# A hybrid decoder step on one Trainium2 core: the list scheduler of layer B makes several passes

## The chip, the cores and the metric

The kernel runs on one core of a Trainium2 chip. The metric is the device time in microseconds of one execution, as the median of several runs. A profile of one further execution shows what each engine did: PE is TensorE, DVE is VectorE, ACT is ScalarE, POOL is GpSimd, and SP is SyncE, whose queue issues all the transfers of this kernel.

## What is computed

One inference step of two layers, for a prompt of 1024 tokens and 64 sample tokens (8 sequences of 8) beside it, with D = 1024. Layer A is a gated short convolution. Layer B is a gated DeltaNet with 8 heads of 128 x 128 state, scanned in chunks:

```
def gdn_mixer(u, conv_buf, s0, w_in, w_conv, a_log, dt_bias, norm_w, w_out):
    p = u @ w_in
    qkv, new_buf = causal_dwconv(p[..., :GDN_CONV_CH], conv_buf, w_conv)
    qkv = jax.nn.silu(qkv).astype(f32)
    ...
    q = l2norm(...); k = l2norm(...); v = ...
    beta = jax.nn.sigmoid(b)
    g = -jnp.exp(a_log) * jax.nn.softplus(a + dt_bias)
    o, S = gated_delta_rule(q, k, v, g, beta, s0)
    o = o * lax.rsqrt(jnp.mean(o * o, axis=-1, keepdims=True) + NORM_EPS) * norm_w
    return (o.reshape(...) * jax.nn.silu(z)) @ w_out, new_buf, S

def gated_delta_rule(q, k, v, g, beta, s0):      # per head and chunk
    L = where(causal, exp(G_i - G_j), 0);  A = where(strict, (k beta) k^T * L, 0)
    u, w = solve(I + A, [v beta, k beta exp(G)]);  attn = (q k^T) * L
    # scan over the chunks
    v_new = u - w @ S;  o = (q exp(G)) @ S + attn @ v_new
    S = S * exp(G_last) + kt^T @ v_new
```

After each layer stands x = layer_norm(ALPHA * x + gate * out).

## The kernel before

Wide products are made from three float32r matmuls: each operand is split into a high and a low part (`uh`, `ul` for the activations in three groups of 384, 384 and 320 columns; `wh`, `wl` for the weights), and hi*hi, lo*hi and hi*lo go into one PSUM bank. A unit of layer B is 24 such matmuls into a bank `g`. The weights of a unit come in halves through one raw buffer `wr`: a load, then two splits on ACT (`wh`) and on DVE (`wl`), then the next load.

Each head has two halves of 512 tokens, and each half is a chain (`prep`): transposes of k (`kq`), the sum of squares on ACT, a power on POOL and three small DVE steps for 1/norm, the normalised keys `kn`, their transpose `KN`, the products KN*KN and KN*kq, from which DVE makes `AT` and `att` with the decay matrix `Lt`. Then the triangular inverse is built in six levels of small matmuls in fp16: 12 products of `DH` and `AH`, 8 products with a unit matrix `id16` that turn a block (`flip`), 12 products of `YH` and `EH`, with DVE and ACT between them. The even and odd half use the banks `t0` and `t1`; their buffers are named with 0 and 1, and with 2 for the samples. A `scan` follows: for each of four chunks the products S*KN, R*E and vn*kt in bank `s`, each ended by one DVE step, and the two products of the output in bank `o`. `norm_out` sums squares, makes f = 1/norm in the same way (ACT, POOL, DVE), and PE transposes the scaled output (`s<-cons,qg`). The samples of a pair of heads go through `sample`: 32 small products of the stored state `S0` with the sample keys `vx`, in two rounds, each round after two loads `S<-in_s_dram`.

The decay matrices are made at the start of layer B (`gates`): `Gc` is transposed on PE, stored to `d_rows`, loaded back as broadcast rows into `rb` and `E`, put through Exp on ACT, stored to `d_L`, and loaded as `Lt`. Exp and Silu need different tables on ACT.

The output projection of layer B (`out_proj`) follows; its first products are put among the last scans.

What sets the order: the kernel's code calls each operation once, and `Plan.add` records it with its price (`Plan.price`: time on the engine, and time until others see the result), what it needs (`deps`) and what it must only follow (`behind`). PE instructions of one output go together as a unit. `Plan.arrange` then schedules the recorded middle of layer B: it gives each unit the length of the longest way to the end, steps through time, gives each of five queues (T = PE, V, A, G, D = SP) the ready unit with the longest way, and ties the queue's instructions in that order. `Plan.on` is set from `gates` to the end of the last head; layer A and the output projections are not recorded. The steps of the change are in `Plan.price`, `Plan.add` and `Plan.arrange`, and in a new `Plan.order`.

## Time and profile before

| | |
|---|---|
| median of 3 runs | 1360.61 us (1359.68 to 1361.13) |
| profiled execution, time | 1356.89 us |
| profiled execution, span | 1355.1 us |
| busy: PE / PEld / DVE / ACT / POOL | 97% / 88% / 61% / 48% / 15% |
| granted clock of PE, mean | 0.994 |

PE is busy nearly all the time. Matmuls are pipelined and their recorded ends overlap, so for PE the distance from one start to the next is read, and what it waits for before an instruction. The recorded middle of layer B lies between about 560 us and 1251 us of the span; layer A is ahead of it, the rest of the output projection behind it.

### The profile page before, as it was taken

The numbers are of one execution on the slowest core, as the hardware profiler recorded it, in microseconds if no ns is written. First come the engines' busy times: TensorE is split into PE (matmuls) and PEld (weight loads), VectorE is DVE, ScalarE is ACT, GpSimd is POOL, SyncE is SP. The second block draws the span as 40 slices with busy tenths as digits, with TensorE's granted clock in tenths as the row PEclk, the third lists the DMA queues.
The fourth block names the chain that finished last, engine by engine and source line by source line (L and its number), as shares of the span: only waits on it lengthen the run. The fifth ranks groups of instructions, "written<-read, shape, count | busy, mean of one in ns | idle before, by whom it ended". The sixth has DMA issues, their size and how long they took to land.

```text
span 1355.1 us, 27508 instructions
## 1 busy us (share of the span) xinstructions
PE 1309.0 (97%) x10631; PEld 1197.4 (88%) x10631; DVE 831.9 (61%) x2010; ACT 652.9 (48%) x1878; POOL 209.4 (15%) x326
## 2 busy tenths in 40 slices
PE   7999999999999999898999999999999999998997
PEld 5898889999999777798999899999999899996775
DVE  3444143244233688667866877787787667557687
ACT  3411212222221355478965768676776567445321
POOL 0011000000000144211121212130303102001041
PEclk9999999999999999999999999999999999999999
DMA  8735542221212332246331232222222224336852
GB/s 310 265 126 190 223 135 77 87 83 68 86 65 68 123 125 88 73 130 187 118 101 50 67 111 80 67 74 88 67 84 83 89 71 129 113 130 202 252 177 68
DMA packets 119023, 160.22 MB, mean 118 GB/s; under 512 B 21220, under 2 KB 74220, under 8 KB 116844
## 3 DMA queue, kind: packets, MB, share of 16 engines
q1 hardware_dynamic: 118892, 158.46, 36.3%
q8 instruction: 83, 1.36, 0.4%
q14 instruction: 48, 0.39, 0.1%
HBM read 123.61 MB, written 34.82 MB: 117 GB/s over the span
## 4 chain that ended last, share of the span: by engine, by line
PE 44%; DVE 7%; DMA 4%; ACT 2%; issue 1%; POOL 1%; SPq 0%; POOLq 0%; ACTq 0%; DVEq 0%
PE g L106 24%; PE t L106 13%; PE s L106 5%; PE o L106 3%; DVE acc L106 1%; DMA S<-in_s_dram 1%; DVE xt L106 1%; DVE wl L106 1%; DMA E<-d_rows 1%; DMA rb<-d_rows 1%; DMA wr<-in_wb_dram 0%; DMA wr<-d_y 0%; DVE Y L106 0%; POOL f1y L106 0%; DVE st L106 0%
## 5 line engine op out<-in xcount | busy, mean ns | idle before, releaser
L106 PE MATMUL g<-uh,wh 128*128 128x384 f32 (+3 forms) x1080 | 376.2, 352 | 1.1 <-DVE wh L106 0.8
L106 PE MATMUL g<-ul,wh 128*128 128x384 f32 (+3 forms) x1080 | 355.1, 332 | 0.0
L106 PE MATMUL g<-uh,wl 128*128 128x384 f32 (+2 forms) x1064 | 350.6, 333 | 0.2 <-DVE wl L106 0.2
L106 DVE TENSOR_TENSOR wl<-wr,wh 128x256 fp32r<-128x256 f32 (+1 forms) x225 | 133.6, 610 | 178.1 <-ACT wh L106 177.9
L106 ACT ACTIVATE wh<-wr 128x256 fp32r<-128x256 f32 (+2 forms) x227 | 109.3, 501 | 213.6 <-PE t L106 118.1
L106 PEld LDWEIGHTS g<-uh,wh 128*128 128x128 f32 (+1 forms) x1080 | 202.2, 187 | 6.1 <-issue 1.2
L106 PEld LDWEIGHTS g<-ul,wh 128*128 128x128 f32 (+1 forms) x1080 | 202.1, 187 | 2.8
L106 PEld LDWEIGHTS g<-uh,wl 128*128 128x128 f32 x1064 | 199.4, 188 | 2.7 <-DVE wl L106 0.5
L106 PE MATMUL t<-uh,wh 128*128 128x384 f32 (+3 forms) x540 | 177.7, 336 | 4.1 <-ACT uh L106 2.9
L106 PE MATMUL t<-ul,wh 128*128 128x384 f32 (+3 forms) x540 | 177.1, 335 | 0.1
L106 PE MATMUL t<-uh,wl 128*128 128x384 f32 (+2 forms) x532 | 173.7, 333 | 0.3 <-DVE wl L106 0.3
L106 DVE SCALAR_TENSOR_TENSOR acc<-xb,wbc,acc 128x512 f32<-128x512 f32 (+1 forms) x144 | 113.8, 792 | 19.1 <-ACT acc L106 18.5
L106 PEld LDWEIGHTS t<-uh,wh 128*128 128x128 f32 (+1 forms) x540 | 101.4, 188 | 16.0 <-issue 6.3
L106 PEld LDWEIGHTS t<-ul,wh 128*128 128x128 f32 (+1 forms) x540 | 101.8, 188 | 5.1 <-issue 2.1
L106 PEld LDWEIGHTS t<-uh,wl 128*128 128x128 f32 x532 | 100.3, 189 | 3.6 <-issue 0.8
L106 ACT ACTIVATE xb<-g 128x384 f32<-128x384 f32 (+4 forms) x122 | 49.7, 413 | 78.8 <-PE g L106 77.7
L106 ACT ACTIVATE EH<-t 128x256 f16<-128x256 f32 (+1 forms) x176 | 57.0, 365 | 5.4 <-PE t L106 4.7
L106 ACT ACTIVATE DH<-t 128x256 f16<-128x256 f32 (+1 forms) x128 | 46.6, 384 | 23.3 <-PE t L106 22.3
L106 PE MATMUL t<-DH,AH 128*128 128x64 f16 x1176 | 52.3, 193 | 1.5 <-DVE DH L106 0.9
L106 PEld LDWEIGHTS <-AH 128*128 128x128 f16 x1176 | 43.4, 98 | 9.9 <-issue 7.2
L106 PEld LDWEIGHTS <-EH 128*128 128x128 f16 x1120 | 41.9, 98 | 9.6 <-issue 4.3
L106 ACT ACTIVATE YH<-Y 128x256 f16<-128x256 f32 (+1 forms) x104 | 41.7, 402 | 17.1 <-DVE Y L106 15.2
(361 smaller groups left out, 2377.7 us busy)
## 6 DMA issues: line engine op xcount, KB each, us to landing
wm<-in_wm_dram SPq DMA_DIRECT2D x16, 1024.0 KB
wr<-in_wb_dram SPq DMA_DIRECT2D x64, 256.0 KB
wr<-in_wa_dram SPq DMA_DIRECT2D x62, 256.0 KB
wm<-in_wm_dram SPq DMA_DIRECT2D x16, 512.0 KB
wr<-d_y SPq DMA_DIRECT2D x32, 256.0 KB
S<-in_s_dram SPq DMA_DIRECT2D x32, 256.0 KB
d_y<-cs SPq DMA_DIRECT2D x8, 544.0 KB
wr<-in_wo_dram SPq DMA_DIRECT2D x16, 256.0 KB
```

The source lines that it names most:

```text
L106: r = call(*args, **kw)
```

## The change

Four things change, all in the planner; the set of operations that the kernel issues stays the same, apart from the table loads of ACT that the order asks for.

1. `arrange` no longer makes one pass. It ranks the units by the longest way, schedules (`order`), schedules the reversed graph from the end with the start times of that pass as ranks, takes the starts of the reversed pass as the next ranks, and so on, six times; the forward pass with the smallest planned end is used.
2. On T, `order` keeps to the class of the last unit (fp16, or anything else) while a ready unit of that class has a rank at most `STAY` = 4.0 below the best one. A change from fp16 to another class is priced at 0.08 (before: 0.078 for a change from any other class to float32r).
3. A transfer is priced at size / rate on its queue, with the rate by the length of contiguous runs, and 2.0 until it is seen (before: 0.06 on the queue, 2.0 + size / 300e3 until seen).
4. Small operations on V and G are priced a little higher; a scale operand on A a little lower; `bn_stats` gets a price of its own, though no recorded part uses it.

```
+    STAY = 4.0
+    PASSES = 6
...
-    V = ((1, 0.155), (128, 0.345), (256, 0.41), (512, 0.69), (1112, 1.34))
-    G = ((1, 0.25), (128, 0.4), (512, 1.3), (1112, 2.65))
+    V = ((1, 0.18), (128, 0.345), (256, 0.41), (512, 0.69), (1112, 1.34))
+    G = ((1, 0.3), (128, 0.4), (512, 1.3), (1112, 2.65))
...
         if kind == "D":
-            return 0.06, 2.0 + min(x.free_size() for x in outs + ins) * P * 4 / 3e5
+            size = min(x.shape[0] * x.free_size() for x in outs + ins) * 4
+            run = min((x.ap[-1][1] if x.ap[-1][0] == 1 else 1) for x in outs + ins) * 4
+            rate = 340e3 if run >= 2048 else 300e3 if run >= 1024 else 200e3 if run >= 512 else max(8e3, run * 300.0)
+            return max(0.06, size / rate), 2.0
+        if kind == "V" and name == "bn_stats":
+            return 0.05 + 0.00106 * ins[0].free_size(), 0.115
...
+            wide = 2 if x.dtype == F32R else x.dtype != F16
...
+    def order(cls, kinds, cost, edges, rank):
...
+            if k == "T":
+                if (kinds[top[1]][1] == 0) != (state[k] == 0):
+                    top = min((x for x in w if (kinds[x[1]][1] == 0) == (state[k] == 0) and x[0] <= top[0] + cls.STAY), default=top)
+                if kinds[top[1]][1] and not state[k]:
+                    t += 0.08
+                state[k] = kinds[top[1]][1]
...
+        best = None
+        for _ in range(cls.PASSES):
+            r = cls.order(kinds, cost, ahead, rank)
+            if best is None or r[0] < best[0]:
+                best = r
+            start = cls.order(kinds, cost, back, {u: t + cost[u][0] for u, t in r[1].items()})[1]
+            rank = {u: t + cost[u][0] for u, t in start.items()}
```

Three places of PE's order, all in the last head.

PE, the last fp16 products of the last sample inverse (bank `t0`, buffers with 2) among a scan step (`s`) and products of the output projection (`t1`), before:

```order
L106 LDWEIGHTS EH2_16393
L106 MATMUL t0_16514<-YH2_16489,EH2_16393 128x64
L106 MATMUL s_16563<-R_16542,E1_16335 128x128
L106 MATMUL t1_16879<-uh0_99,wh_16829 128x512
L106 LDWEIGHTS DH2_16392
L106 MATMUL t0_16554<-id16_76,DH2_16392 128x64
L106 MATMUL t1_16879<-ul0_102,wh_16829 128x512
L106 LDWEIGHTS DH2_16392
L106 MATMUL t0_16554<-id16_76,DH2_16392 128x64
L106 MATMUL t0_16618<-S0_16595,vx_16591 32x128
```

and the same two products `t0_16554` after:

```order
L106 MATMUL o_16286<-vn_16475,att0_15263 128x128
L106 MATMUL s_16498<-vn_16475,kt0_15150 128x128
L106 LDWEIGHTS DH2_16392
L106 MATMUL t0_16554<-id16_76,DH2_16392 128x64
L106 LDWEIGHTS DH2_16392
L106 MATMUL t0_16554<-id16_76,DH2_16392 128x64
L106 MATMUL t0_16618<-S0_16595,vx_16591 32x128
```

Three runs of fp16 products, each followed by another class, stand in the first piece; the second has one.

PE, what stands between the first and the second round of the last sample state products (`t0_16618`, `t0_16665`), before:

```order
L106 MATMUL t0_16618<-S0_16597,vx_16591 32x128
L106 MATMUL s_16577<-vn_16565,kt1_15302 128x128
L106 MATMUL g_16840<-uh0_99,wh_16823 128x512
L106 MATMUL g_16841<-uh0_99,wh_16823 128x512
L106 MATMUL g_16840<-ul0_102,wh_16823 128x512
L106 MATMUL g_16841<-ul0_102,wh_16823 128x512
L106 MATMUL g_16840<-uh0_99,wl_16824 128x512
L106 MATMUL o_16539<-S_16500,qg1_15233 128x128
L106 MATMUL o_16539<-vn_16565,att1_15391 128x128
L106 MATMUL s_16603<-cons_75,qg0_15108 128x128 x4
L106 MATMUL g_16841<-uh0_99,wl_16824 128x512
L106 MATMUL g_16840<-uh0_99,wh_16823 128x512
```

and after, the last eleven rows ahead of the second round:

```order
L106 MATMUL t1_16334<-EH1_15447,YH1_16259 64x64
L106 MATMUL g_16841<-uh0_99,wl_16824 128x512
L106 MATMUL g_16840<-uh1_100,wh_16823 128x512
L106 MATMUL g_16841<-uh1_100,wh_16823 128x512
L106 MATMUL s_16563<-R_16542,E1_16335 128x128
L106 MATMUL g_16840<-ul1_103,wh_16823 128x512
L106 MATMUL g_16840<-uh1_100,wl_16824 128x512
L106 MATMUL g_16841<-ul1_103,wh_16823 128x512
L106 MATMUL g_16841<-uh1_100,wl_16824 128x512
L106 MATMUL s_16577<-vn_16565,kt1_15302 128x128
L106 MATMUL t0_16665<-S0_16637,vx_16591 32x128
```

Ahead of these, behind the first round, the second order also has one scan product, the 12 products and 8 flips of a level of `t1`, five output products `g` and three more among the 12 small products of `t1_16334`.

PE, from the last output product of the last scan (`o`) to the transposes of the last norm (`s_16776`), before:

```order
L106 MATMUL o_16539<-vn_16702,att1_15391 128x128
L106 MATMUL s_16708<-vn_16702,kt1_15302 128x128
L106 MATMUL t1_16879<-ul0_102,wh_16829 128x512
L106 MATMUL t1_16878<-uh0_99,wl_16830 128x512
L106 MATMUL t1_16879<-uh0_99,wl_16830 128x512
L106 MATMUL t1_16878<-uh1_100,wh_16829 128x512
L106 MATMUL t1_16879<-uh1_100,wh_16829 128x512
L106 MATMUL t1_16878<-ul1_103,wh_16829 128x512
L106 MATMUL t1_16879<-ul1_103,wh_16829 128x512
L106 MATMUL t1_16878<-uh1_100,wl_16830 128x512
L106 MATMUL t1_16879<-uh1_100,wl_16830 128x512
L106 MATMUL s_16776<-cons_75,qg1_15233 128x128 x4
```

and after:

```order
L106 MATMUL o_16539<-vn_16702,att1_15391 128x128
L106 MATMUL s_16708<-vn_16702,kt1_15302 128x128
L106 MATMUL t1_16878<-uh1_100,wl_16830 128x512
L106 MATMUL t1_16879<-uh1_100,wl_16830 128x512
L106 MATMUL s_16776<-cons_75,qg1_15233 128x128 x4
```

Nine products of the output projection stand between the two before, and two after; the other seven now stand ahead of the scan's last steps.

## Rows read from the trace of the kernel before

**Rows 1.** Stages: length, busy us (count) of PE, PEld, DVE, ACT, POOL, then clock.

```profile
588.00:700.00 112.00, 107.02 (x1034) 101.01 (x1035) 86.11 (x227) 97.30 (x252) 19.65 (x37) 1.00 0.48 147
700.00:1220.00 520.00, 513.38 (x5611) 487.63 (x5610) 375.37 (x991) 342.74 (x1175) 90.74 (x180) 1.00 0.28 87
```

**Rows 2.** PE's waits, 560 to 1250 us: total, times, longest.

```profile
PE t L106 <- DMA S<-in_s_dram: 3.8, 3, 1.9
PE t L106 <- DVE kn L106: 2.2, 3, 1.0
...
PE g L106 <- DVE wl L106: 0.2, 1, 0.2
```

**Rows 3.** PE in order of time: start, us, instruction, count.

```profile
1204.31 0.38 PE L106 MATMUL s<-vn,kt 128*128 128x128 f32 x2
1204.53 0.39 PE L106 MATMUL o<-vn,att 128*128 128x128 f32 x2
...
1205.53 0.42 PE L106 MATMUL g<-uh,wh 128*128 128x384 f32 x1
1205.79 0.34 PE L106 MATMUL g<-ul,wh 128*128 128x384 f32 x1
1205.96 0.34 PE L106 MATMUL g<-uh,wl 128*128 128x384 f32 x1
1206.14 0.38 PE L106 MATMUL s<-S,KN 128*128 128x128 f32 x2
1206.28 0.42 PE L106 MATMUL g<-uh,wh 128*128 128x384 f32 x1
1206.54 0.33 PE L106 MATMUL g<-ul,wh 128*128 128x384 f32 x1
...
1207.25 0.47 PE L106 MATMUL s<-R,E 128*128 128x128 f32 x2
1207.55 0.40 PE L106 MATMUL t<-id,DH 128*128 128x64 f16 x8
```

**Rows 4.** The two rounds of the last sample's state products: PE, and SP's issue.

```profile
1228.58 1.08 PE L106 MATMUL t<-S,vx 128*32 128x128 f32 x32
1229.75 0.94 SPq L106 DMA_DIRECT2D S<-in_s_dram  x2
1234.46 0.38 PE L106 MATMUL t<-S,vx 128*32 128x128 f32 x2 [1.86 <-DMA S<-in_s_dram]
1080.86 0.38 PE L106 MATMUL t<-S,vx 128*32 128x128 f32 x2 [1.61 <-DMA S<-in_s_dram]
```

**Rows 5.** The last norm on PE.

```profile
1245.15 0.45 PE L106 MATMUL o<-vn,att 128*128 128x128 f32 x2
...
1246.35 0.62 PE L106 MATMUL t<-uh,wh 128*128 128x512 f32 x2
1246.81 0.63 PE L106 MATMUL t<-ul,wh 128*128 128x512 f32 x2
...
1250.78 0.76 PE L106 MATMUL s<-cons,qg 128*128 128x128 f32 x4 [2.88 <-DVE qg L106]
```

**Rows 6.** ACT's table loads: by form, 560 to 1250 us; two rows in time.

```profile
L106 ACT ACT_TABLE_LOAD x20 | 25.7, 1283 | 0.3
599.71 1.28 ACT L106 ACT_TABLE_LOAD   x1
601.00 0.64 ACT L106 ACTIVATE rb<-rb 128x512 f32<-128x512 f32 x1
```

**Rows 7.** Start of layer B: a decay load and its reader, a weight load and its.

```profile
606.62 0.32 SPq L106 DMA_DIRECT2D Lt<-d_L  x1
617.14 0.60 DVE L106 SCALAR_TENSOR_TENSOR AT<-t,bsc,Lt 128x128 f32<-128x128 f32 x2
611.90 0.38 SPq L106 DMA_DIRECT2D wr<-in_wb_dram  x1
616.02 0.72 ACT L106 ACTIVATE wh<-wr 128x256 fp32r<-128x256 f32 x2 [1.13 <-DMA wr<-in_wb_dram]
```

More of the change, by code (lines that the diff above doesn't have):

```diff
@@ L259, in arrange, with tie @@
     @classmethod
+    def order(cls, kinds, cost, edges, rank):
+        import heapq
+        left, ready = dict.fromkeys(cost, 0), dict.fromkeys(cost, 0.0)
+        for u in cost:
+            for v, _ in edges[u]:
+                left[v] += 1
+        coming, waiting = ({k: [] for k in "TVAGD"} for _ in range(2))
+        free, state, queue, start = dict.fromkeys("TVAGD", 0.0), {"T": 2, "A": 0}, {k: [] for k in "TVAGD"}, {}
+        for u in cost:
+            if not left[u]:
+                heapq.heappush(coming[kinds[u][0]], (0.0, u))
+        for _ in cost:
+            t, k = min((free[k] if waiting[k] else max(free[k], coming[k][0][0]), k) for k in "TVAGD" if waiting[k] or coming[k])
+            w = waiting[k]
+            while coming[k] and coming[k][0][0] <= t:
+                u = heapq.heappop(coming[k])[1]
+                heapq.heappush(w, (-rank[u], u))
+            top = w[0]
+            if k == "T":
[4 more added lines that the diff above has]
+                state[k] = kinds[top[1]][1]
+            elif k == "A" and kinds[top[1]][2]:
+                t += 1.28 * (kinds[top[1]][2] != state[k])
+                state[k] = kinds[top[1]][2]
+            if top is w[0]:
+                heapq.heappop(w)
+            else:
+                w.remove(top)
+                heapq.heapify(w)
+            u = top[1]
+            start[u], free[k] = t, t + cost[u][0]
+            queue[k].append(u)
+            for v, lag in edges[u]:
+                ready[v] = max(ready[v], t + lag)
+                left[v] -= 1
+                if not left[v]:
+                    heapq.heappush(coming[kinds[v][0]], (ready[v], v))
+        return max(start[u] + sum(cost[u]) for u in cost), start, queue
+    @classmethod
     def arrange(cls, tc):
-        import heapq
         cls.on = False
-        def order(i, j):
+        def tie(i, j):
             tc.add_manual_dep(i, j.name, mybir.DependencyInfo(mybir.DependencyClass.NoSync, mybir.DependencyReason.DATA), reason="order")
@@ L277, in arrange @@
                 if nodes[d][0] != v[0]:
-                    order(v[1], nodes[d][1])
-        after, follow = ({u: [] for u in units} for _ in range(2))
+                    tie(v[1], nodes[d][1])
+        kinds = {u: (nodes[u][0], nodes[u][6], nodes[u][7]) for u in units}
+        cost = {u: (sum(nodes[i][4] for i in units[u]), max(nodes[i][5] for i in units[u])) for u in units}
+        ahead, back = ({u: [] for u in units} for _ in range(2))
         for u in units:
-            deps[u].discard(u)
-            behind[u] -= deps[u] | {u}
-            for d in deps[u]:
-                after[d].append(u)
-            for d in behind[u]:
-                follow[d].append(u)
-        cost = {u: (sum(nodes[i][4] for i in units[u]), max(nodes[i][5] for i in units[u])) for u in units}
-        left = {u: len(deps[u]) + len(behind[u]) for u in units}
+            lags = {d: 0.0 for d in behind[u]}
+            lags.update((d, sum(cost[d])) for d in deps[u])
+            lags.pop(u, None)
+            for d, lag in lags.items():
+                ahead[d].append((u, lag))
+                back[u].append((d, cost[u][0] + lag - cost[d][0]))
+        rank = {}
+        left = {u: len(back[u]) for u in units}
         line = [u for u in units if not left[u]]
         for u in line:
-            for v in after[u] + follow[u]:
+            for v, _ in ahead[u]:
                 left[v] -= 1
@@ L295, in arrange @@
         assert len(line) == len(units)
-        way = {}
         for u in reversed(line):
-            way[u] = max(sum(cost[u]) + max((way[v] for v in after[u]), default=0.0), max((way[v] for v in follow[u]), default=0.0))
-        left = {u: len(deps[u]) + len(behind[u]) for u in units}
-        ready = dict.fromkeys(units, 0.0)
-        coming, waiting = ({k: [] for k in "TVAGD"} for _ in range(2))
-        free, last = dict.fromkeys("TVAGD", 0.0), dict.fromkeys("TVAGD", None)
-        state = {"T": True, "A": 0}
@@ new lines, in arrange @@
+            rank[u] = max((rank[v] + lag for v, lag in ahead[u]), default=sum(cost[u]))
+        best = None
[5 more added lines that the diff above has]
+            rank = {u: t + cost[u][0] for u, t in start.items()}
+        for queue in best[2].values():
+            line = [i for u in queue for i in units[u]]
+            for i, j in zip(line, line[1:]):
+                tie(nodes[j][1], nodes[i][1])
```

32 lines of the change are left out of this document (2 added, 30 removed).

## The prediction

> **What bounds the kernel now.** I read the stages first, then who waited for whom, then stretches of PE in order of time. PE is recorded busy for 107.0 of 112 us at the start of the recorded middle of layer B and for 513.4 of 520 us in the bulk of it [rows 1], so PE sets the time there. The change does not take a matmul away. It can therefore win in two ways only: where a matmul starts later than the one before it allows without any wait (a cost of the order itself), and where PE waits.
>
> The first is seen in the stretch of single instructions [rows 3]. A wide product takes 0.17 to 0.18 us from start to start (1205.79, 1205.96, 1206.14). The wide product at 1205.53, which follows fp16 products, has its successor 0.26 us later. After a fp32 product this costs nothing: from s<-S,KN at 1206.14 to the second wide product at 1206.54 are 0.40 us, which is 0.22 for the two passes of the fp32 product (1204.31 to 1204.53) and 0.18 for a wide one. A fp32 product after fp16 is slow too: s<-R,E at 1207.25 takes 0.30 us to the next start, where 0.22 is usual. So each step from fp16 to either other class costs PE about 0.08 us, and no other step does.
>
> The waits between 560 and 1250 us come to 12.9 us in fourteen kinds, of which the first, the second and the last are shown [rows 2]: 3.8 us are waits for the sample states, 9.1 us are small waits of up to 1 us for DVE and ACT steps of the chains. One more of 2.88 us comes at the end, before the transposes of the last norm [rows 5].
>
> **Fewer changes of class.** In the program's order the fp16 products stand in 235 uninterrupted runs before and in 157 after; the first pair of pieces of order shows how. That is 78 changes x 0.08 us = **6.2 us** less on PE, and PE is the bound. The price is read at both kinds of change, so I take it whole; the lower bound is 0, if PE only waits instead, which is a rival below.
>
> **The sample states.** The second round of the state products needs two loads into buffers that the first round frees. Last sample: the first round runs from 1228.58 to about 1229.4 (recorded ends overlap), the next two loads are issued at 1229.75, and PE goes on at 1234.46 [rows 4]. That is 5.1 us from round to round. Before, PE has 2.7 us of work there: 0.22 for s<-vn,kt, 7 wide products of 512 columns at 0.23 (1246.35 to 1246.81, two of them, [rows 5]), two fp32 products at 0.22 and four transposes at 0.11 (half a fp32 product). 2.7 + the wait of 1.9 and some issue time makes the 5.1. After, the second pair of pieces and what stands ahead of them hold 15 wide products (3.5 us), three fp32 products (0.66), 32 fp16 products (1.0 at 0.03; eight of them at 1207.55 take at most 0.40 together [rows 3]) and some four changes of class (0.3): 5.4 us. The wait ends there. For the third sample, whose wait is 1.61 us [rows 4] and some 0.4 behind it, the same count gives 3.1 us before and 5.3 after. I take **3.4 us** of the 3.8, with bounds of 0 (the loads come later on SP, behind a store that waits) and 3.8.
>
> **The small waits.** Here only the order can be read, so I counted how much PE work, at the starts' distances above, lies between a result of PE and the product that needs what the other engines make of it. From the transposes of k to those of kn the four shortest of 16 were 6.3, 7.0, 7.4 and 7.5 us and become 6.4, 7.1, 7.7 and 8.0. From the first flip to the first level 7 of 16 lay under 1.55 us, now 1. From YH*EH to the next DH*AH 18 of 84 lay under 1.5 us, now 10. Between two steps of a scan 46 of 168 lay under 0.9 us, now 33. Against that, two steps DH*AH to YH*EH of the last head fall to 1.35 to 1.5 us, where the shortest was 1.56. So half of the 9.1 us should go, **4.5 us**, and new ones of **1.5 us** come; bounds from all 9.1 gained to 5 lost, the latter if as many places turn tight as were eased.
>
> **The last norm.** Its chain (squares on ACT, power on POOL, DVE) takes from the last o<-vn,att at 1245.15 to 1250.78, of which the PE work between covers 9 x 0.23 + 0.22 = 2.3 us and 2.88 is waited [rows 5]. After, 2 x 0.23 + 0.22 = 0.7 us stand there [third pair of pieces], so the wait grows by **1.6 us**; bounds 0 (if DVE, which does a split of the output weights in between, comes sooner) and 2.3. The seven products that moved ahead lengthen the gaps of the scan, where they cover its steps; that is in the small waits.
>
> **The rest of the change.** The transposes of Gc, from which all decay matrices come, now stand behind 51 wide products instead of 15, 6.2 us of PE work later, while the first AT products move back by 2.7 us only. Cover: the first Lt is issued at 606.62, needs some 4 us (a weight load issued at 611.90 is used at 616.02) and is first read at 617.14 [rows 7], so 6.5 us are spare, and 3.5 are used up. Without cover it would cost up to 3.5. The order asks for four more table loads on ACT, 4 x 1.283 = 5.1 us [rows 6]. They stand among the last of the exponentials, at or just behind the end of the first stage, where ACT is idle 14.7 of 112 us, and 177 of 520 behind it [rows 1]; I cost them at 0, with 5.1 if they were on the path. The new prices of bn_stats and of small operations add no instruction: 0.
>
> The Trainium skill ("ScalarE: Activation LUTs", What ACT_TABLE_LOAD costs) speaks against the change here: it counts a drain of about 1.38 us with each load, 2.66 us a switch. By it the four would cost ACT an estimated 10.6 us. The trace does not agree: the load at 599.71 ends at 600.99 and the exponential starts at 601.00, and 0.3 us of idle time stand before all twenty [rows 6]. The sum is the same by either, since ACT's idle time covers both.
>
> **Sum.** -6.2 - 3.4 - 4.5 + 1.5 + 1.6 = -11.0 us. From the profiled execution, 1356.9, that gives 1345.9. That execution was 3.7 us under the median of the runs, so the median should come to 1360.6 - 11.0 = **1349.6 us**, 0.8% less.
>
> **Rivals.** (a) *PE waits instead.* The chains through DVE and ACT, not PE, set the pace, above all in the first stage, where ACT is busy 97.3 of 112 us [rows 1]; what PE saves it then waits. For: ACT's load there. Against: 520 us of bulk with DVE at 72% and ACT at 66%, and PE recorded busy 99%. Then the 6.2 and the 4.5 are lost and the states' 3.4 less 1.6 and 1.5 remain: 1360.3, no change. If only the small waits stay, 1354.1, which I count to the forecast. Chance 0.16.
>
> (b) *More goes.* Nearly all 9.1 us vanish and no new waits come: -6.2 - 3.8 - 8 + 1.6 = -16.4, 1344.2 us. For: almost every count of cover above rises. Against: a planned order is only as good as its prices, and the trace's loads take 4.1 us where the plan has some 2.8. Chance 0.14.
>
> (c) *Slower: the weight loads.* There is one raw buffer, so a load, two splits and the next load follow one another, and a late one stops 24 wide products. The plan now counts 0.77 us on the queue and 2.0 until seen for a load of 256 KB; the row shows 4.1 us from issue to use, 1.13 of it waited by ACT [rows 7]. If the tighter order has each of the 13 halves of the first stage (26 splits of ACT) come 1.3 us late on PE, 17 us are lost: 1349.6 + 17 = 1366.6 us. It decides against the change from 9 late loads on. Against: the old price was as short, and PE waited only 0.2 us for wl [rows 2]; the new order issues weight loads earlier among the stores. Chance 0.10.
>
> (d) *The forecast*, 1345 to 1356 us: 0.60.
>
> **How the numbers follow.** About 0.2%, 2.7 us, is what a measurement of this kernel can tell from no change. Faster by more than that, below 1357.9: (d), (b) and a quarter of (a), 0.78. Within: most of (a) and a little of (c), 0.13. Slower: 0.09. The range leaves out the far end of (b), since all bounds at their best give 1360.6 - 6.2 - 3.8 - 9.1 = 1341.5, and the slow part of (a) and (c): 1342.5 to 1359.
>
> **What would show it.** Right: the waits for S<-in_s_dram under 0.6 us in all; PE's starts 0.26 us apart behind fp16 some 78 times fewer; the end of the last norm's transposes some 11 us earlier than 1250.8, with a wait of about 4.5 us before them; the stretch behind it, 105 us, unchanged. Wrong: new waits for wl or for AT at 600 to 650 us; waits for YH and DH that sum to more than before; the bulk as long as now. What would undo the forecast is above all that PE is idle in new places for as long as it was spared.

## The result and the profile after

The changed kernel takes 1341.28 us, median of 4 executions (1339.32 to 1341.79), against 1360.14 us of the kernel before in the same comparison: ratio 0.986, 95% interval 0.9843 to 0.9877. In a second comparison it took 1340.5 us against 1356.73 (ratio 0.9876, 0.9854 to 0.9898). So it is faster by 16 to 19 us where 11.0 were forecast, and the first 1341.28 lies 1.2 us under the low end of the forecast's range. The profiled execution took 1341.3 us with a span of 1339.5; its span is 15.6 us shorter than the 1355.1 before.

Stages of the kernel after, with the columns of [rows 1]; the second window ends at nearly the same work as before (14 matmuls fewer), some 15 us earlier:

```profile
587.00:699.00 112.00, 109.21 (x1034) 105.06 (x1033) 89.05 (x228) 102.33 (x257) 17.58 (x35) 1.00 0.47 145
699.00:1205.00 506.00, 503.67 (x5597) 481.87 (x5595) 379.28 (x989) 342.74 (x1175) 87.23 (x182) 1.00 0.31 90
```

In the first stage PE does as many matmuls in 112 us as before and sits idle for 2.8 us of it where it was 5.0 [rows 1]. The bulk holds 14 matmuls fewer in 14 us less, with 2.3 us idle in place of 6.6.

PE's waits of the kernel after, 560 to 1250 us (total, times, longest), to be held against [rows 2]:

```profile
PE s L106 <- DVE qg L106: 5.1, 2, 4.9
PE t L106 <- DVE kn L106: 1.6, 1, 1.6
PE t L106 <- DVE DH L106: 1.4, 3, 0.6
PE o L106 <- DVE vn L106: 1.1, 1, 1.1
```

The line that stood first before, S<-in_s_dram with 3.8 us, is gone, and so is the 1.0 us for AT. The list of eight lines comes to 11.0 us, of which 4.9 are the one wait of the last norm; before it was 12.9 and the 2.88 of [rows 5]. The rounds of the last sample, the answer to [rows 4] (start, us, instruction, count):

```profile
1210.30 1.08 PE L106 MATMUL t<-S,vx 128*32 128x128 f32 x32
1211.47 0.99 SPq L106 DMA_DIRECT2D S<-in_s_dram  x2
1217.64 1.08 PE L106 MATMUL t<-S,vx 128*32 128x128 f32 x32
```

From start to start the two rounds now lie 7.3 us apart, where it was 5.9 [rows 4]. By the prediction's measure, from the end of the first, that is some 6.5 us, where it had counted 5.4. PE has work all that time, and waits for nothing ahead of the second round.

A run of fp16 products and what follows it, the answer to [rows 3]:

```profile
1179.91 0.87 PE L106 MATMUL t<-YH,EH 128*128 128x64 f16 x24
1180.62 0.42 PE L106 MATMUL g<-uh,wh 128*128 128x384 f32 x1
1180.88 0.34 PE L106 MATMUL g<-ul,wh 128*128 128x384 f32 x1
1181.05 0.35 PE L106 MATMUL g<-uh,wl 128*128 128x384 f32 x1
```

The step from fp16 costs what it cost: 0.26 us to the next start (1180.62 to 1180.88) where 0.17 is usual. But the run behind it is long: the next fp16 product comes at 1184.93, 27 wide products later.

The last norm of the kernel after, the answer to [rows 5]:

```profile
1230.23 0.49 PE L106 MATMUL o<-vn,att 128*128 128x128 f32 x2 [1.14 <-DVE vn L106]
1230.56 0.39 PE L106 MATMUL s<-vn,kt 128*128 128x128 f32 x2
1230.70 0.71 PE L106 MATMUL t<-uh,wl 128*128 128x512 f32 x2
1236.30 1.12 PE L106 MATMUL s<-cons,qg 128*128 128x128 f32 x4 [4.89 <-DVE qg L106]
1237.07 0.78 PE L106 MATMUL o<-uh,wh 128*128 128x512 f32 x1
1237.64 0.63 PE L106 MATMUL o<-ul,wh 128*128 128x512 f32 x1
1238.07 0.63 PE L106 MATMUL o<-uh,wl 128*128 128x512 f32 x1
```

The transposes start 14.5 us earlier than before, behind a wait that is 2.0 us longer. The last rows show something the prediction did not look for: the wide products behind the wait start 0.43 us apart (1237.64, 1238.07), where the same shape took 0.23 [rows 5]. Three windows there, first of the kernel after, then of the kernel before (columns of [rows 1]; the number behind POOL is the granted clock):

```profile
1231.50:1236.30 4.80, 0.00 (x0) 0.00 (x1) 3.05 (x10) 2.40 (x10) 1.02 (x1) 0.81 0.21 60
1236.30:1241.40 5.10, 5.10 (x14) 4.21 (x15) 1.29 (x2) 1.91 (x5) 0.00 (x0) 0.51 0.48 141
1241.40:1244.00 2.60, 2.60 (x13) 2.13 (x12) 0.79 (x2) 0.79 (x3) 0.00 (x0) 1.00 0.00 0
```

```profile
1247.90:1250.80 2.90, 0.03 (x1) 0.03 (x1) 2.64 (x8) 1.90 (x5) 1.02 (x1) 1.00 0.92 279
1250.80:1254.30 3.50, 3.50 (x11) 2.87 (x12) 2.48 (x4) 2.15 (x6) 0.00 (x0) 0.56 0.59 188
1254.30:1257.00 2.70, 2.70 (x12) 2.21 (x11) 0.00 (x0) 0.09 (x1) 0.00 (x0) 0.94 0.43 121
```

In the kernel after, the granted clock falls to half (1.2 of 2.4 GHz) within the wait (0.81 on the mean of it) and stays there for 5.1 us of work; in the kernel before it falls as the wait ends and stays down for 3.5 us. By an estimate from these windows about half of that is lost: 2.5 us and 1.5 us. The Trainium skill ("TensorE: Matmul & The Clock Gate", Terms) prices a stretch at the low clock in the same way, at its length times the share of pulses withheld; the starts 0.43 us apart agree.

ACT's table loads, the answer to [rows 6], and three rows of the first stage, for [rows 7] and for the longest wait there:

```profile
L106 ACT ACT_TABLE_LOAD x24 | 30.8, 1283 | 0.4
```

```profile
609.06 0.32 SPq L106 DMA_DIRECT2D Lt<-d_L  x1
...
614.17 0.63 PE L106 MATMUL t<-cons,kn 128*128 128x128 f32 x4 [1.57 <-DVE kn L106]
...
617.56 0.80 DVE L106 SCALAR_TENSOR_TENSOR AT<-t,bsc,Lt 128x128 f32<-128x128 f32 x2 [3.54 <-PE t L106]
```

Four more loads at 1283 ns, with 0.4 us of idle time ahead of all 24; the first Lt is issued 8.5 us before its reader, and that reader waits for PE, not for the load. By these rows neither costs PE anything, as forecast. The drain that the Trainium skill counts with each load ("ScalarE: Activation LUTs", What ACT_TABLE_LOAD costs) shows in no row of either kernel.

**Where 15.6 us went.** I took the distance from each PE start to the next, less the usual distance of that shape (0.1755 us for 384 columns, 0.148 for 320, 0.229 for 512, 0.222 for a fp32 product, 0.029 for a fp16 one). What is over behind a step out of fp16 is booked to the change of class, up to 0.085 us; what is over by more than 0.15 us elsewhere is a wait; the rest is small. From the first gate product of layer B (`t<-gg`) to the last norm's transposes:

```
                      before            after
usual distances       608.8             609.2
changes of class       17.1 (236)        10.8 (158)
waits                  21.2 (30 places)  14.4 (19)
  sample states         4.4               0
  last norm             3.0               5.1
  all others           13.8               9.3
small rest             16.1              14.9
sum                   663.3             649.2
```

That is 14.1 us. The stretch ahead of it is 0.4 us shorter, and this is no gain: three wide products of 320 columns that stood there now stand in the stretch of the table. Behind it 1.1 us are gained (104.3 us to the end before, 103.2 after). By starts a wait is longer than its row says: the others' 13.8 us before have 9.1 recorded, the 9.3 after have 6.1, 0.18 us more for each place both times.

This compares one profiled execution with one. The profiled execution of the second comparison, of the same changed kernel, spans 1341.7 us, of which 650.9 are the stretch of the table, 1.7 more than in the first. So 1 or 2 us between single profiles, here and in the tables below, are no more than two executions of one kernel differ by.

### The profile page after: what moved, and what is told of

Its sections match the earlier page's. It is cut to its first block, busy times and chain, and to the rows that moved or that the text cites. A ratio compares the mean times of both kernels' runs of the same rounds, so it can differ in the third digit from the quotient of the medians.

```text
span 1339.5 us, 27506 instructions
## 1 busy us (share of the span) xinstructions
PE 1299.6 (97%) x10631; PEld 1194.4 (89%) x10631; DVE 836.2 (62%) x2010; ACT 656.5 (49%) x1882; POOL 200.8 (15%) x326
## 5 line engine op out<-in xcount | busy, mean ns | idle before, releaser
L106 DVE TENSOR_TENSOR wl<-wr,wh 128x256 fp32r<-128x256 f32 (+1 forms) x225 | 136.3, 618 | 171.3 <-ACT wh L106 170.9
L106 DVE SCALAR_TENSOR_TENSOR acc<-xb,wbc,acc 128x512 f32<-128x512 f32 (+1 forms) x144 | 114.2, 793 | 25.5 <-ACT acc L106 24.4
L106 ACT ACTIVATE EH<-t 128x256 f16<-128x256 f32 (+1 forms) x176 | 58.1, 365 | 25.3 <-PE t L106 24.4
L106 DVE TENSOR_TENSOR Y<-t,cons 128x256 f32<-128x256 f32 (+1 forms) x104 | 41.2, 404 | 17.0 <-PE t L106 16.8
L106 DVE TENSOR_TENSOR YH<-Y,YH 128x256 f16<-128x256 f32 (+1 forms) x104 | 43.3, 420 | 4.1 <-ACT YH L106 3.8
```

The lines of the kernel that those rows point to most:

```text
L106: r = call(*args, **kw)
```

## Experiments

Theory T, taken from the prediction and these numbers: the time is the usual distances, 0.08 us for each change of class, and the waits. Rival A is the prediction's: what PE saves it then waits. Theory O says that executions without the profiler wait longer for loads than the profiled one, to explain why the first three executions of before lay 3.7 us above it. Expectations count "short places": steps YH*EH to DH*AH and DH*AH to YH*EH with under 1.5 us of PE work between them, and scan steps with under 0.9.

### The parts of the change, one and two at a time

Each kernel is the changed one with some of its parts put back. The four edits are:

```diff
-    STAY = 4.0
+    STAY = -1.0
-    PASSES = 6
+    PASSES = 1
-            return max(0.06, size / rate), 2.0
+            return 0.06, 2.0 + min(x.free_size() for x in outs + ins) * P * 4 / 3e5
-    V = ((1, 0.18), ...
-    G = ((1, 0.3), ...
+    V = ((1, 0.155), ...
+    G = ((1, 0.25), ...
```

The fourth has one line more, which puts a scale operand on ACT back from 0.1 to 0.11. Three things stay as changed in every kernel here: the price of `bn_stats`, which no recorded part uses, the price of a change of class, and the three classes of units that go with it.

`none` has all four; `only_stay`, `only_passes` and `only_prices` keep one part (the prices are the third and the fourth edit together), `no_stay`, `one_pass` and `old_prices` lack one.

> The new planner's code with every number put back: no patience on TensorE (STAY -1), one pass from the front, the old prices of loads, bn_stats and small operations. Its order has 232 changes from fp16 to another class behind the first gg product (before 236, after 158), 3.5 and 2.7 us of PE work between the last two samples' state rounds (before 3.1 and 2.7), and 54 places of YH to DH and of the scans that are short of cover (before 66, after 46). Theory T (nominal PE work, 0.08 us for each change of class, waits at the sample states, small waits of some 0.24 us for each short place): 1341.3 + 5.9 + 2 + 3.8 for the states - 1.6 for the last norm, about 1351. Theory O (executions without the profiler wait some 3.3 us longer for the samples' loads than the profiled one did, so the kernel before is 1360 and not 1356.9): about 1354 to 1356. Rival (the code itself, its units of three classes in place of two, brings the gain): about 1343.

> TensorE's patience alone (STAY 4, one pass, old prices). 176 changes of class, a gap of 2.7 us at the last sample's states, 64 short places, 1.1 us of work before the last norm. Theory T: 1341.3 + 1.4 + 4 + 2.4 - 0.4 = 1348 to 1349. Theory O: 1350 to 1352. Rival A (what the changes of class cost comes back as waits): 1355 or more.

> The six passes alone (no patience, old prices). 236 changes of class; the samples' gaps are 3.4, 3.5 and 3.2 us in three of four places, so some 5.2 us are waited there; 47 short places. Theory T: 1341.3 + 6.2 + 5.2 - 0.2 = 1352.5. Theory O: 1355 to 1357, 3 to 4 us above its profiled execution. Rival A: 1346.

> The new prices alone (no patience, one pass). 236 changes of class, the samples' gaps at 5.2, 5.2 and 6.8 us, 55 short places, 3.1 us of work before the last norm. Theory T: 1341.3 + 6.2 + 1.7 - 2.4 = 1347. Theory O: 1347 too, with the time within 1 us of its profiled execution. Rival A: 1341.

> The changed kernel without TensorE's patience (STAY -1): six passes and new prices stay. 238 changes of class again (after 158), the samples' gaps all at 5.2 us or more, fewer short places than after (42 against 46). Theory T: 1341.3 + 80 x 0.08 = 6.4, small waits -1.2, the last norm's wait 2.4 less (3.1 us of work stand before it in place of 0.7): 1344. Rival A (PE waits in place of what the changes of class cost): 1338, below the changed kernel. Theory O: 1344 as well, since no load is waited for.

> The changed kernel with one pass only. 176 changes of class (+1.4 us), 55 short places (+1.7), the samples' gaps at 5.0 us or more, 3.1 us of work before the last norm (-2.4). Theory T: 1342. If the passes are what shortens the waits: 1345 or more.

> Patience and six passes with the old prices. 153 changes of class, only 33 short places (after 48), but gaps of 4.7 and 3.6 us at the samples' states (1.9 us waited), 1.6 us before the last norm. Theory T: 1341.3 - 0.4 - 3.6 + 1.9 - 0.9 = 1338. Theory O: 1340 to 1342. If the prices are worth what the sample states waited (3.8 us by the profile of the kernel before): 1345.

Measured, with the account of the stretch up to the last norm by starts, in us:

```
              median    ratio to before (95%)   changes: us   waits (places)
none          1353.14   0.9966 (0.9952-0.998)   232: 16.8     19.5 (28)
only_stay     1350.87   0.9942 (0.9926-0.9957)  176: 12.2     23.0 (32)
only_passes   1359.88   1.0014 (1.0001-1.0027)  236: 17.4     27.5 (29)
only_prices   1354.70   0.9973 (0.9959-0.9987)  236: 17.5     17.9 (23)
no_stay       1346.18   0.9913 (0.9894-0.9932)  238: 17.2     11.2 (22)
one_pass      1346.17   0.9909 (0.9891-0.9927)  176: 11.9     16.5 (24)
old_prices    1354.83   0.9969 (0.9956-0.9982)  153: 10.8     26.8 (37)
```

**What `none` keeps.** It is itself 4.7 us faster than the kernel before (0.9966, interval below 1), some quarter of the whole gain, with nearly as many changes of class and 1.7 us less of waits, which is within what two profiles of one kernel differ by. Of the change as described it keeps the price of a change of class, with the classes of units, and the new code itself. Part of the difference goes with the clock: its executions have 0.995 on the mean, those of the kernel before beside it 0.993. These kernels do not take that quarter apart any further.

**Changes of class.** Patience is worth 3.3 us on top of none (0.9966 to 0.9942, times 1358), 8.7 on top of the prices (0.9973 to 0.9909 with one pass), 6.1 on top of the passes, and 5 to 7 as the last part (0.9913 to 0.9876 or 0.986). The counts fall by 56, 60, 83 and 80. By medians that is 0.06 to 0.15 us for each change that goes, since the waits move as well. The account, which books at most 0.085, gives 0.066 to 0.074 us for a change in every kernel here and below, from 138 to 238 of them. Rival A falls for the most part: with 238 changes `no_stay` waits least of these seven, and is still some 5 us behind the changed kernel. Of the 6.4 us that patience saves there in changes, 3.2 do come back as waits (14.4 in place of 11.2), but 2.8 of these are the wait of the last norm alone (4.89 us in place of 2.10).

**Passes and prices work only together.** With the old prices six passes cost 6.7 us (none to only_passes); with the new ones they gain 8.5 (only_prices to no_stay). The new prices alone change nothing that can be measured (none to only_prices). Taking them back under the six passes costs 13 to 15 us (0.9969 against 0.9876 and 0.986). Here my expectation was wrong by most: by counts of PE work `old_prices` has the best cover of all and should have been the fastest at 1338 us. Counts in PE's order see no transfer: in `only_passes` and `old_prices` alike PE waits 4.5 and 4.8 us in one place of the first stage, behind a weight load that comes late (below).

**Theory T's size.** It is within 2.5 us for `none`, `only_stay` and `no_stay`, and 4 to 17 us too low for the other four. What it lacks is waits that no count had shown, and with them goes a lower clock: 0.990 to 0.992 in the mean of the executions of these four, 0.993 to 0.995 in `none`, `only_stay` and `no_stay`.

**Theory O falls.** `only_passes` waits 2.3 us for sample states and should have had 3 to 4 us between its profiled execution (1359.83) and the median (1359.88); `only_prices`, which does not, has 0.4. That `none` and `only_stay` came out nearer to its figures than to those of T is no support for it, as T starts from the one measured 1341.3 and is too low throughout.

### More of it

```diff
-    STAY = 4.0
-    PASSES = 6
+    STAY = 8.0
+    PASSES = 24
```

> More of the same: patience of 8 in place of 4, 24 passes in place of 6. 150 changes of class, 47 short places, a gap of 4.0 us at the last sample's states, 3.0 us before the last norm. Theory T: 1341.3 - 0.6 + 1.1 - 2.3 = 1339 to 1340. Rival A: 1342 or more, the longer patience makes chains late.

1335.73 us, ratio 0.9835 (0.9818 to 0.9852), 150 changes of class and 13.5 us of waits. By medians it is 3 us beyond the expected 1339 to 1340. But its profiled execution, at a mean granted clock of 0.993, took 1341.36, as the changed kernel does at that clock; those of 1335.6 to 1335.7 have 0.996 and 0.997, and one of 1339.6 has 0.996 too. So it is not shown that more patience and more passes gain anything beyond the clock that went with these executions.

### The clock, and the kernel before once more

> The changed kernel once more, beside more executions of the kernel before. So far all four of its executions had a mean granted clock of 0.993; the kernel before had 0.989 to 0.997 in 29 executions, and its time fell by about 1 us for each 0.001 of it. Theory C (3 to 4 us of the measured 18.9 are the clock that the first three executions of before drew): the ratio comes out at 0.987 to 0.988, a gain of 16 to 17.5 us, and the executions order by their clock. If the gain is 18.9 us in truth: ratio 0.986, and no tie to the clock.

1340.5 us (1338.48 to 1343.45) against 1356.73, ratio 0.9876, a gain of 16.2 us, as theory C had it. Its executions at a clock of 0.994 took 1338.5 to 1340.5 us, those at 0.992 and 0.993 1341.1 and 1343.5. The tie is loose: the four of the first comparison, all at 0.993, took 1339.3 to 1341.8. All 88 executions of the kernel before that stood beside the experiments have a median of 1357.5 us; four of the ten levels of clock among them:

```
granted clock   executions   mean us
0.991            7           1359.6
0.993           13           1358.9
0.995           18           1356.7
0.997            4           1354.1
```

The slope over all 88 is 0.86 us for 0.001, with a correlation of -0.67: under half of the spread of 1352 to 1363 us goes with the clock. Nor is the clock a cause by itself. In the profile of the kernel before, its mean of 0.994 is made of four stretches at half clock: three behind waits of PE (from 497, 558 and 1251 us on), one at the end, where PE has no more work. So a wait that happens to be longer can lower the clock as well as lengthen the time, and these numbers don't tell which came first. What they do tell is the level: the first three executions, with a median of 1360.6 (their clock is not on record), were a high draw from this spread, and the profiled one (1356.89, clock 0.994) was an ordinary one.

The next kernel keeps PE busy at the one place where the change made it idle for longer, with products that nobody reads:

```diff
             f = rsqrt(r["pool"], so[:, :nu], nu, "f%d" % x)
+            if r.get("id") == (H - 1, 1):
+                ps = psc.tile([P, 4 * P], F32, name="s")
+                for i in range(16):
+                    T.matmul(ps, lhsT=wo[0][0][:, :P], rhs=wo[0][0][:, :4 * P], start=True, stop=True)
             os_ = r["qg"]
```

> The changed kernel with 16 wide products of 512 columns whose result nobody reads, put between the last scan and the transposes of the last norm: 3.7 us of work where TensorE was idle for 4.9 us and the granted clock then stood at 0.50 until 5.1 us behind it. The planner moves other work as well (166 changes of class, 5.0 us of work before the transposes in place of 0.7). Theory C (idle time lowers the clock and so is paid twice): clock 1.00 behind the transposes, the wait under 1 us, 2.5 us gained there and 0.6 lost by changes: 1339. If the clock falls there for another reason: still 0.50 behind the transposes, 1341 to 1342.

1336.31 us, ratio 0.9849 (0.9825 to 0.9873), 4.2 us less than the changed kernel beside it, with intervals that still overlap. PE there:

```profile
1233.48 3.81 PE L106 MATMUL s<-uh 128*128 128x512 f32 x16
1237.14 0.48 PE L106 MATMUL o<-uh,wh 128*128 128x512 f32 x1
1237.46 0.60 PE L106 MATMUL s<-cons,qg 128*128 128x128 f32 x4
1237.81 0.48 PE L106 MATMUL o<-ul,wh 128*128 128x512 f32 x1
1238.13 0.40 PE L106 MATMUL t<-vx,att 128*128 128x512 f32 x1
1238.37 0.40 PE L106 MATMUL o<-uh,wl 128*128 128x512 f32 x1
1238.60 0.40 PE L106 MATMUL o<-uh,wh 128*128 128x512 f32 x1
```

The stretch behind it, to the end of the output projection (columns of [rows 1]):

```profile
1237.50:1327.00 89.50, 88.52 (x410) 71.39 (x408) 74.31 (x149) 21.58 (x52) 19.66 (x18) 1.00 0.57 183
```

The transposes wait for nothing, the wide products behind them are 0.23 us apart at once, and the clock is 1.00 all the way: with the idle time the low clock is gone. What that is worth is not to be had from this pair. In the profiled executions (spans of 1339.5 and 1335.5 us) 2.2 of the 4.0 us lie ahead of the first gate product, which starts at 587.08 and 584.92 us; up to there PE has the same order in both, so this is the spread between executions. And the planner placed other work anew too (8 more changes of class, waits of 11.6 us in 24 places). The clearer pair stands at the end, `more_small` and `all_small16`.

### The prices

> The changed kernel with the old price of DMA alone (0.06 us on the queue for any load). Eight row loads of 256 KB stand ahead of the second weight load of the first stage, as in old_prices, where that load took 6.6 us and TensorE waited 4.8 us for what comes behind it. Theory L (the price of loads is what old_prices lacked): 1350 to 1355, a wait of 4 to 5 us at 608 to 613. By counts of changes of class (159) and short places (40) alone: 1338 to 1339.

> The changed kernel with the old prices of bn_stats and of small operations, and the new price of DMA. Three row loads stand ahead of the second weight load (after: one). 154 changes of class, 40 short places, a gap of 3.8 us at the last sample's states, 3.7 us of work before the last norm. Theory L: within 2 us of the changed kernel, 1339 to 1343. If the small prices carry the 13 us that old_prices lost: 1348 or more.

`old_load` took 1363.51 us (ratio 1.0042, 1.0026 to 1.0058), slower than the kernel before, and 23 us slower than the changed kernel beside it (1340.5). `old_small` took 1336.23 (0.9843, 0.9819 to 0.9867): the new prices of small operations bring nothing; without them it was 4.3 us faster by medians, though the intervals overlap. (Its expectation names `bn_stats` too, but the edit leaves that price as changed.) SP's issues at the start of layer B in `old_load`, ACT's wait there, and PE's:

```profile
599.06 0.82 SPq L106 DMA_DIRECT2D rb<-d_rows  x2
599.92 0.91 SPq L106 DMA_DIRECT2D E<-d_rows  x2
600.87 1.85 SPq L106 DMA_DIRECT2D qg<-d_rows  x4
602.82 0.75 SPq L106 DMA_DIRECT2D wr<-in_wb_dram  x1
...
609.08 0.42 ACT L106 ACTIVATE wh<-wr 128x256 fp32r<-128x256 f32 x1 [5.96 <-DMA wr<-in_wb_dram]
...
613.80 0.64 PE L106 MATMUL g<-uh,wh 128*128 128x320 f32 x1 [4.78 <-ACT xb L106]
```

and the same of the changed kernel:

```profile
599.95 0.35 SPq L106 DMA_DIRECT2D rb<-d_rows  x1
601.44 0.33 SPq L106 DMA_DIRECT2D wr<-in_wb_dram  x1
...
604.43 0.41 ACT L106 ACTIVATE wh<-wr 128x256 fp32r<-128x256 f32 x1
```

At 0.06 us a load, the planner puts eight row loads of 256 KB right ahead of the weights, and the weight load takes 6.3 us from issue to use in place of 3.0. ACT waits in its order for the split, and PE for the copy xb that stands behind it on ACT. The Trainium skill ("DMA: Bandwidth & Descriptors", Two DMAs through the same engine are not ordered) has it that the pieces of transfers start in order within one queue of one DMA engine. A load that takes 6.3 us behind eight others agrees with that. But this stall is one of many. Windows of `old_load`, then of the changed kernel, up to 1185 us:

```profile
587.00:640.00 53.00, 46.77 (x311) 45.77 (x312) 33.22 (x91) 37.95 (x98) 5.97 (x12) 0.94 0.51 167
640.00:699.00 59.00, 55.07 (x604) 51.98 (x603) 46.85 (x116) 48.93 (x130) 13.31 (x25) 0.97 0.36 121
699.00:1185.00 486.00, 479.71 (x5307) 458.12 (x5306) 362.59 (x950) 329.12 (x1137) 85.03 (x176) 1.00 0.27 84
```

```profile
587.00:640.00 53.00, 51.42 (x392) 50.39 (x391) 40.90 (x100) 47.89 (x115) 7.50 (x14) 1.00 0.52 158
640.00:699.00 59.00, 57.78 (x643) 54.67 (x643) 48.15 (x129) 54.44 (x143) 10.08 (x21) 1.00 0.44 134
699.00:1185.00 486.00, 483.67 (x5421) 463.09 (x5419) 367.19 (x960) 333.24 (x1147) 86.33 (x179) 1.00 0.30 88
```

`old_load` loses 7.4 us of PE in the first stage (and has a clock of 0.94 and 0.97 there), and 4.0 in the bulk. By starts it waits 32.9 us in 50 places up to the last norm, against 14.4 in 19, and its stretch behind the last norm is 4.1 us longer (107.4 against 103.2).

Three more kernels price some loads as new and all others as old:

```diff
+            if not (...):
+                return 0.06, 2.0 + min(x.free_size() for x in outs + ins) * P * 4 / 3e5
             size = min(x.shape[0] * x.free_size() for x in outs + ins) * 4
```

where the condition is, in turn: an input named d_rows (`rows_price`), an output named wr (`wr_price`), either (`rows_wr`).

> The changed kernel with the new price of DMA for the row loads alone (those from d_rows); every other load is priced as before the change. One row load stands ahead of the second weight load of the first stage (after: one; old_load: eight, 1363.5 us). 158 changes of class, 36 short places, a gap of 3.4 us at the last sample's states, 3.5 us of work before the last norm. Theory R (the rows at the weight loads are what the old price spoils): 1338 to 1343, no wait of 4 to 5 us at 608 to 613. If the price of the other loads carries it: 1350 or more, with the small waits of old_load (33 us in some 50 places) and without its stall at 608.

> The changed kernel with the new price of DMA for the weight loads alone (those into wr); every other load is priced as before the change. Eight row loads stand ahead of the second weight load of the first stage again. If the weight loads carry what the row loads do not (rows_price 1354, old_load 1363.5, the changed kernel 1340.5): about 1350, with the stall at 608. If the rest lies with other loads (decay matrices, sample states, z and stores): 1358 or more.

> The new price of DMA for row loads and weight loads together, the old one for all others. 157 changes of class, a gap of 3.4 us at the last sample's states, 3.5 us of work before the last norm, 38 short places. If these two kinds carry the price of loads: 1338 to 1343. If the others carry the rest: 1350 or more, as rows_price.

```
              median    ratio to before (95%)   waits (places)
rows_price    1354.37   0.9977 (0.9966-0.9989)  24.2 (40)
wr_price      1344.99   0.9921 (0.9906-0.9937)  13.1 (17)
rows_wr       1346.24   0.9931 (0.9909-0.9954)  18.7 (35)
old_load      1363.51   1.0042 (1.0026-1.0058)  32.9 (50)
```

By ratio the price of row loads brings 9 us of 23 and that of weight loads 16; both together bring 15. None of my three expectations held in full: the parts don't add up, and `wr_price` has no stall at 608 us though eight row loads stand ahead of its second weight load as well. Its last four row loads, the weight load, and what ACT does before the split:

```profile
597.91 1.86 SPq L106 DMA_DIRECT2D qg<-d_rows  x4
601.38 0.33 SPq L106 DMA_DIRECT2D wr<-in_wb_dram  x1
608.13 0.20 ACT L106 ACTIVATION_READ_ACCUMULATOR junk<-t 128x1 f32 x1
608.22 0.42 ACT L106 ACTIVATE wh<-wr 128x256 fp32r<-128x256 f32 x1
```

ACT does not wait for this load: it has other work up to the split. The row loads also go out some 3 us earlier than in `old_load`, and the weight load is issued 1.6 us behind the last of them instead of at once (602.82). In the kernel before, with the old price, eight row loads stand ahead too, and the weight load follows 3.3 us behind the last, at 602.42; PE's longest wait from 600 to 612 us is 0.3 us. So it is not the number of loads ahead that makes the stall. Whether it is gone because the plan knows the time of the weight load, or because of where the order happens to put the rows, these kernels don't part. The longest wait of `wr_price` in that stage is 3.0 us, for kn. Which of the small waits comes from which load, I could not settle.

### Putting them together

```diff
-    STAY = 4.0
-    PASSES = 6
+    STAY = 8.0
+    PASSES = 24
-    V = ((1, 0.18), ...
-    G = ((1, 0.3), ...
+    V = ((1, 0.155), ...
+    G = ((1, 0.25), ...
+                for i in range(16):
+                    T.matmul(ps, lhsT=wo[0][0][:, :P], rhs=wo[0][0][:, :4 * P], start=True, stop=True)
```

This is `all_small16`. `fill_small16` keeps patience at 4 and six passes, `more_small` lacks the 16 products.

> The changed kernel with the products that nobody reads before the last norm (as in fill) and with the old prices of bn_stats and of small operations (as in old_small). 152 changes of class, 37 short places, 6.6 us of work before the last norm, a gap of 4.4 us at the last sample's states. By the terms fill - 0.08 x 14 - 0.24 x 11, + 1 for the states: 1333 to 1335. If the two gains are the same one (both move work ahead of the last norm): 1336.

> Patience 8 and 24 passes with the new price of DMA and the old prices of small operations. 143 changes of class (after 158), 35 short places (after 48), but 0.5 us of work before the last norm and a gap of 2.7 us at the last sample's states. By the terms: 1340.5 - 1.2 - 3 + 2.5 = 1339, with the granted clock at 0.50 behind the last norm, as in the changed kernel. If counts of cover say nothing beyond the changed kernel: 1341.

> All that helped: patience 8, 24 passes, the new price of DMA, the old prices of small operations, and 16 products that nobody reads before the last norm. 138 changes of class, 36 short places, 6.4 us of work before the last norm, a gap of 4.4 us at the last sample's states. By the terms, against fill (1336.3): -0.08 x 28 = -2.2, small waits -2.9, states +1: 1332. If what the patience saves comes back as waits: 1336.

```
               median    ratio to before (95%)   changes: us  waits (places)  mean clock
fill_small16   1335.97   0.9837 (0.9819-0.9856)  152: 10.3     8.0 (14)       0.995
more_small     1341.93   0.9882 (0.9863-0.9901)  143:  9.7    14.0 (14)       0.993
all_small16    1333.29   0.9821 (0.9804-0.9838)  138:  9.1     9.4 (18)       0.995
```

`fill_small16` came out at what was expected if the gains of `fill` and `old_small` are one and the same. `more_small` lies at what was expected if counts of cover say nothing; it has 0.5 us of work before the last norm where `old_small` has 3.7, and waits 4.9 us there. `all_small16` is 8.6 us faster than it, where by the terms 7 were expected; the intervals lie apart, and the two edits differ in the 16 products alone. Behind the last norm the clock is 0.53 in `more_small` (1236 to 1242 us) and 1.00 in `all_small16` (1235 to 1245 us). The planner moves other work with them here too, so the 8.6 us are those of the edit, not of the clock alone; in the two profiles 3.0 us lie ahead of the first gate product, as with `fill`. It is the fastest kernel here, 24.4 us under the kernel before, some 7 under the changed one; from `fill`, `fill_small16`, `old_small` and `more` its interval does not part it.

## Why the prediction was wrong

Its sign, its places and the bulk of its reasons held; its size did not. 8.3 us lie between 1349.6 and 1341.3, in two parts: 3.7 us that it added at the end, and 4.6 us of the sum (15.6 less 11.0).

**The offset, 3.7 us: the step "so the median should come to".** It took the median of three executions as the level and the profiled one as low. With 88 executions the median is 1357.5, and the profiled one took 1356.9. From there the same sum gives 1346.5. Taken from there, the low end of the range would have been 1339.4 in place of 1342.5. Part of the spread goes with the granted clock, for which the prediction looked at the stage windows alone, where it reads 1.00 [rows 1].

**Changes of class, 6.2 forecast, 6.3 by starts.** Right in count (236 to 158), in price (0.07 us by starts) and in that it is paid in time, as `no_stay` with its 238 changes shows; half of it came back as waits, nearly all in the last norm, which the sum has as a term of its own.

**The sample states, 3.4 forecast, 4.4.** Right in kind: no wait for S is left. The term was sized by recorded idle time of 3.8; the distance of starts shows 4.4.

**The small waits, net 3.0 forecast, 4.5.** By recorded waits the net is 3.0 exactly (9.1 to 6.1), which is luck: the second profile of the changed kernel has 7.1, a net of 2.0. Mis-sized was the unit: recorded spans of matmuls overlap, and a wait costs PE some 0.18 us more than its row. The counts of cover were right in sign here by luck more than by method: in `old_prices` they were 17 us off.

**The last norm, +1.6 forecast, +2.0.** The wait came as forecast, 4.9 us for 4.5. What the prediction missed is that the clock falls with such a wait and PE pays again behind it, an estimated 2.5 us now for 1.5 before; in `fill`, without the wait, it does not fall.

**Costed at nothing.** The later Gc transposes and the four more table loads: right, by the rows above. The stretch behind the last norm was to stay: it gained 1.1 us (0.4 by the second profile of the changed kernel), as waits for wh of 1.1 and 1.0 us shrank to one of 0.5 us, which outweighs 1.0 us more of low clock. The small rest (1.2) was not in the sum; what it is made of is not shown. "The new prices add no instruction: 0" was harmless for the sum, since the counts were taken from an order that held them, but wrong as a reading of the change: what a price adds is another order. Taken back, that of the small operations changes nothing clear of noise (`old_small`), and that of DMA alone costs 23 us and turns the result.

**The rivals.** (a) fell for the most part with `no_stay`. (b), more goes, at 1344.2, was nearest. (c), late weight loads, did not come. `old_load` shows its kind, one late weight load that stops PE for 4.8 us. That its time, 1363.5 us, lies near the 1366.6 of (c) is chance: the other waits there are for many steps, and not thirteen late halves. (c)'s argument against itself, that the old price was as short, holds for plans of one pass only: of the kernels with the old price, the three with six passes and the old price of all loads (`only_passes`, `old_prices`, `old_load`) have that stop, of 4.5 to 4.8 us.

## What to carry to other kernels

A search over plans, here passes to and fro, can lose with prices that are wrong where it gained with others: check the prices against rows before searching longer, and those of transfers first, since no count of the engine's own order shows a late load. Size waits by the distance of starts, not by recorded idle time, and look at the granted clock behind each longer wait of PE; it may pay to fill it with products that nobody reads. And take the level of a program from many executions with their clocks before a difference of 3 us is explained.

## What the runs showed of the hardware

PE idle for 3 to 5 us was granted 1.2 GHz from the end of that wait or within it, and did 3.5 to 5.1 us of work at that level, with wide products 0.43 us apart in place of 0.23. With products in place of the wait the clock stayed at 1.00. The mean clock of an execution moves from 0.989 to 0.998 for one and the same program; the time goes with it at 0.86 us for each 0.001, with a correlation of -0.67, and which of the two moves the other is not shown. A step from fp16 to another class cost 0.066 to 0.074 us in 19 kernels. A weight load of 256 KB took 3.0 us from issue to use behind one row load and 6.3 us right behind eight.
